# Own buffers for A22, A12 cast behind the copies, and a longer hand-written order at the FFN entry

## The chip, the core and the metric

The kernel runs on one core of one Trainium2 chip. The metric is the time of one execution on the device in microseconds (us), as the median of several runs. TensorE (PE in the profile) multiplies matrices, VectorE (DVE) and ScalarE (ACT) work element by element, GpSimd (POOL) here mostly issues DMAs, and SyncE (SP) issues most of the loads. Each engine takes its instructions in the order in which they were queued.

## What is computed

One layer of a diffusion backbone over 512 latent tokens of width 1024 with a context of 256 tokens: a modulated RMSNorm, one wide input projection, a pooling mixer and a bidirectional mLSTM, a gated sum, an output projection with a residual; then a second modulated RMSNorm, a SwiGLU feed-forward part with its own residual, and a last RMSNorm. The change lies in the feed-forward part (FFN), whose width is 2816, that is 22 tiles of 128:

```python
def _swiglu(h, w_in, w_out):
    g, u = jnp.split(h @ w_in, 2, axis=-1)
    return (jax.nn.silu(g) * u) @ w_out
...
        x = x + g2 * _swiglu(_modulate(x, norm_ffn[l], sh2, sc2), w_ffn_in[l], w_ffn_out[l])
```

All data are 32-bit floats. A product in that precision is made of three matmuls: each operand is split into a high part (a cast, on ACT) and a low part (operand minus high part, a subtraction on DVE), and the kernel adds high x high, high x low and low x high.

## The kernel before, in words

**Tiling.** Tokens lie along the free axis, 512 of them in two halves of 256. For each of the 22 FFN tiles j there are two weight tiles of 128 x 1024 (`wffi[2j]` for the gate, `wffi[2j+1]` for the up branch), eight k-tiles of 128 x 128 in each.

**Plain tiles and Strassen pairs.** FFN tiles 0, 1 and 2 are computed directly by the class `Half`, one half of the tokens at a time: 24 matmuls for `gate`, 24 for `up`, then `silu` on ACT, `product` on DVE, `high` (a cast on ACT) and `low` (a subtraction on DVE). From tile 3 on (`NP = 3`) gate and up tile are handled together as a 2 x 2 block matrix by the class `Pair`, with Strassen's scheme in Winograd's form: seven block products instead of eight. The gate tile holds A11 and A12 (its first and last four k-tiles), the up tile A21 and A22. The seven products use as stationary operands A11, S1, S2, A12, S3, S4 and A22, where S1 and S2 are sums made of A22, A21 and A11 (called sum12 here) and S3 and S4 are sums made of A11, A21, S2 and A12 (sum34). The token side (B11, N1, N2, B21, T3, B22, T4) is prepared once for all pairs. Each product is four k-tiles x three matmuls of 256 tokens, so 12 matmuls; a pair has 84.

**Making the weights of a pair.** The generator `prepare` (L1017) loads the up tile into a buffer `ur` (two of them) and the gate tile into a buffer `wr` (three) over SP's queue. Then come in program order: A11's cast and low part; sum12 (L1054, L1055 on DVE), its cast (L1044 on ACT, into `gh`) and low part (L1045 on DVE, into `gl`); A12; sum34 (L1061, L1062); its cast (into `wh`) and low part (into `wl`); A22. A11, A12 and A22 share the buffers `oh` (high) and `ol` (low), five of each, taken in turn, so a sixth tile waits for the product that reads the first. For A12 and A22 the low part is not made on DVE: ACT writes minus the high-part source into `ol` (L1038) and POOL issues a DMA that adds the weights from memory to it (L1039, an accumulating DMA). In two later pairs A11 goes that way too. An `ur` buffer is free for the next load when its A22 has been read, a `wr` buffer when A11, A12, sum12 and sum34 have read it.

**Order of the products.** A `Pair` has two generators. `front` gives A11 (whose result ACT copies from bank x to bank z, L1091), S1 (whose result ACT copies to a buffer q, L1095; this instruction is `copied`), S2 (added onto x; DVE then adds q, L1098) and A12 (added onto z). `back` gives S3, S4 and A22. S2 may not start before the copy of x to z, since it writes x. The function `run` strings pairs together; in a round the order on PE is A11, S1 of this pair, S3 of the pair before, S2 of this one, S4 before, A12 of this one, A22 before. Before the products of a round, `run` calls `made(after)`, which queues the whole preparation of the next pair.

**What sets the order.** The FFN entry (from L1349) is in a block whose order on PE, ACT and DVE is the program's, written out by hand. Outside such blocks a scheduler at build time orders each engine by program order, dependencies, buffers and its own estimates; DMA queues are always ordered by it. `issue_after(x)` adds an edge: what the block queues on x's engine comes behind x there, without a semaphore. In the entry, the hand-written block ends after A11 and S1 of pair 3 (called `third`) and its preparation; pair 4's preparation and products come from the scheduler.

**Where the pairs lie.** Pairs 3 to 7, then the output product for tiles 0 to 7 (`ffn_out`), then pairs 8 to 13 (`Even` and `Odd`), four `Out` pairs that apply Strassen's scheme to the output weights (their low parts are all made on DVE), pairs 14 to 21, and the rest of the output product. The buffers `oh` and `ol` also hold some weights of the output projection before the FFN (`wo`), of FFN tile 1 and of the last output product.

In the text pair n's operand is written A12(n), S3(n) and so on.

Of the kernel before, what the change touches and what calls it, by code (L numbers as in the profile page):

```python
# [10 lines left out]
F32 = mybir.dt.float32  # L11
# [6 lines left out]
P = 128  # L18
# [13 lines left out]
BUFS = {"a": 16, "ac": 8, "tmp": 7, "kq": 7, "q": 4, "E": 6, "Sp": 10, "m": 7, "pm": 4, "act": 16, "x1": 8, "oh": 5, "ol": 5}  # L32
# [18 lines left out]
def layer_kernel(ctx: ExitStack, tc, xT, cT, w0, w1, wv0, wv, wada_a, wada_b, par, crow, bg, wpool,  # L51
# [811 lines left out]
    for h in range(H):  # L863
# [13 lines left out]
        if h == H - 1:  # L877
            close_pool("att")
            close_pool("kqp")
            open_pool("late1", ("oh", "ol", "gh", "gl"))  # L880
            open_pool("late0", ("act",))
            for j in range(6):
                y_split(j)
# [66 lines left out]
    with tc.issue_after(ylow.ins):  # L950
        wo = {j: wload(wout[j], D, ("oh", "ol") if j < NW + 2 else None)[0] for j in range(NW, KT)}
# [65 lines left out]
    def prepare(p, wa, wb, n, turns, sent, behind=None):  # L1017

        a = tl("wr", [P, WMAX], F32, 3)[:, :2 * n]
        b = tl("ur", [P, D], F32, 2)[:, :2 * n]  # L1020
        p["loaded"] = nc.sync.dma_start(b, wb)
        nc.sync.dma_start(a, wa)

        def tiled(t):
            return t.rearrange("p (k c) -> p k c", c=P) if turns else t

        def parted(t):
            return [tiled(t)[:, e::2] for e in range(2)] if turns else [tiled(t[:, :n]), tiled(t[:, n:])]

        (a11, a12), (a21, a22) = parted(a), parted(b)  # L1030

        def direct(nm, w, dram):
            h, l = S("oh", F32R)[:, :n], S("ol", F32R)[:, :n]
            nc.scalar.copy(tiled(h), w)
            if nm not in sent:
                V.tensor_sub(tiled(l), w, tiled(h).bitcast(F32))  # L1036
            else:
                nc.scalar.activation(tiled(l), w, AF.Copy, scale=-1.0)  # L1038
                p["added"] = nc.gpsimd.dma_start(tiled(l), dram, accum_op=ALU.add)  # L1039
            p[nm] = ptiles(h, l, 0, n)  # L1040

        def summed(names, sg, h, l):
            h, l = h[:, :2 * n], l[:, :2 * n]
            nc.scalar.copy(h, sg)  # L1044
            p["low"] = V.tensor_sub(l, sg, h.bitcast(F32))  # L1045
            for e, nm in enumerate(names):
                p[nm] = ptiles(h, l, e * n, n)

        yield
        s12 = tl("sg", [P, D], F32, 2, LINE)[:, :2 * n]  # L1050
        s1, s2 = tiled(s12[:, :n]), tiled(s12[:, n:])
        direct("A11", a11, parted(wa)[0])
        with tc.issue_after(behind.ins) if behind else ExitStack():
            V.tensor_add(s1, a22, a21)  # L1054
        V.tensor_add(s2, s1, a11)  # L1055
        summed(("S1", "S2"), s12, wide("gh"), wide("gl"))
        yield
        direct("A12", a12, parted(wa)[1])
        yield
        s34 = tl("sg", [P, D], F32, 2, LINE)[:, :2 * n]  # L1060
        V.tensor_add(tiled(s34[:, :n]), a11, a21)  # L1061
        V.tensor_add(tiled(s34[:, n:]), s2, a12)  # L1062
        yield
        summed(("S3", "S4"), s34, *(tl(t, [P, WMAX], F32R, 2, LINE) for t in ("wh", "wl")))
        yield
        direct("A22", a22, parted(wb)[1])
        yield
# [3 lines left out]
    class Pair:  # L1071
# [5 lines left out]
        begun, f, behind = False, None, None  # L1077
# [5 lines left out]
        def prepare(self):  # L1083
            return prepare(self.p, wffi[2 * self.j], wffi[2 * self.j + 1], T, False, self.sent, self.behind)
# [128 lines left out]
    class Out(Pair):  # L1213
# [8 lines left out]
        def prepare(self):  # L1222
            w = [wffo[2 * self.j + e][:, self.c] for e in range(2)]
            return prepare(self.p, *w, (self.c.stop - self.c.start) // 2, True, self.sent)
# [28 lines left out]
    def made(it):  # L1253
        for _ in it.prepare():
            pass

    def run(items, also=lambda it: None):

        prev, casts[:] = None, []
        for it, after in zip(items, items[1:] + [None]):  # L1260
            f = it.f = it.f or it.front()
            if after:
                made(after)
            b = prev.back() if prev else iter(())
# [8 lines left out]
            if casts:  # L1273
                with tc.issue_after(it.copied.ins):
                    casts.pop().cast(0, 4)
# [6 lines left out]
            next(b, None)  # L1282
# [28 lines left out]
    for j in range(2):  # L1311
        d = ("oh", "ol") if j else "wide"
        pw.append((wload(wffi[2 * j], D, d)[0], wload(wffi[2 * j + 1], D, d)[0], act_tiles(j)))
# [35 lines left out]
    with tc.manual_schedule(engines={mybir.EngineType.PE, mybir.EngineType.Activation, mybir.EngineType.DVE}):  # L1349
# [41 lines left out]
        third = Pair(NP, NP)  # L1391
        p = third.prepare()
        next(p)
        next(p)
        e.silu()
        next(p)
# [4 lines left out]
        next(p)  # L1401
# [43 lines left out]
    turn = itertools.count(NP + 1)  # L1445
# [72 lines left out]
    for j, dst in enumerate((None, None, "wide", "wide", ("oh", "ol"), ("oh", "ol"), None, None)):  # L1518
# [117 lines left out]
```

## Time and profile before

| | |
|---|---|
| median of 3 runs | 883.52 us (882.77 to 883.98) |
| the profiled execution's own time | 883.43 us |
| span of its profile, first to last instruction | 881.6 us |
| PE busy | 870.8 us (99%), 6052 matmuls |
| DVE busy | 631.2 us (72%) |
| ACT busy | 454.2 us (52%) |
| POOL busy | 82.6 us (9%) |
| granted TensorE clock, mean | 0.999 |
| moved by DMA | 129.83 MB, mean 147 GB/s |

The span is 1.8 us shorter than the execution's own time; what lies around the span is not in the profile. In the timeline a row gives start and duration in us, engine, line and operation, output<-input by buffer name, and in brackets how long the engine was idle before it and who released it. A matmul's duration includes its way through the pipeline, so matmuls that follow each other without a gap overlap: what tells of a stall is the distance from one start to the next.

### The profile page before, as it was taken

To read this page: it belongs to the slowest core of one execution; us is meant where nothing else is said; L and a number is where in the kernel's file an instruction comes from. 1 tells how busy PE (TensorE), PEld (TensorE's weight loads), DVE (VectorE), ACT (ScalarE), POOL (GpSimd) and SP (SyncE) were. 2 spreads that over 40 slices of the span, in tenths; PEclk is the share of its full clock that TensorE was granted. 3 is DMA by queue.
4 is the path that set the end of the run, shared out by engine and by line. 5 is a ranking of instruction groups with operands and counts; after the bars stand their busy time and mean duration, and the time that the engine had idled before them with its cause. 6 is when DMAs were issued, how large, how long until landed. Compare 5 with 4: busy or idle time off the path is not lost.

```text
span 881.6 us, 15517 instructions
## 1 busy us (share of the span) xinstructions
PE 870.8 (99%) x6052; PEld 800.4 (91%) x6052; DVE 631.2 (72%) x1232; ACT 454.2 (52%) x867; POOL 82.6 (9%) x117
## 2 busy tenths in 40 slices
PE   9999999999999999999999999999999999999996
PEld 8689798899888998889988899999889999999996
DVE  5678677867876688767886667794376898786544
ACT  4464354455344453445454447674146768676431
POOL 0000010020000100000000000020011202322000
PEclk9999999999999999999999999999999999999999
DMA  9853021436252542434354740385476647998502
GB/s 352 326 194 112 25 72 60 169 106 181 72 185 91 152 158 83 148 112 140 127 162 130 266 141 1 89 211 133 131 207 171 150 108 213 219 227 204 168 1 96
DMA packets 45449, 129.83 MB, mean 147 GB/s; under 512 B 5024, under 2 KB 9408, under 8 KB 44352
## 3 DMA queue, kind: packets, MB, share of 16 engines
q1 hardware_dynamic: 37344, 112.59, 39.4%
q0 software_dynamic: 8032, 16.26, 9.5%
q8 instruction: 47, 0.77, 0.3%
q14 instruction: 26, 0.21, 0.1%
HBM read 120.94 MB, written 9.98 MB: 149 GB/s over the span
## 4 chain that ended last, share of the span: by engine, by line
PE 89%; DMA 3%; ACT 2%; DVE 2%; issue 2%; DVEq 0%; POOLq 0%; POOL 0%; SPq 0%; ACTq 0%
PE ps L191 12%; PE ps L192 12%; PE ps L193 12%; PE ps L201 8%; PE ps L199 8%; PE ps L198 8%; PE pat L351 3%; PE ps L582 3%; PE ps L583 3%; PE ps L584 3%; PE pat L192 2%; PE pat L193 2%; PE pat L191 2%; PE pat L796 2%; PE pat L797 2%
## 5 line engine op out<-in xcount | busy, mean ns | idle before, releaser
L161 ACT CAST wh<-wr 128x1024 fp32r<-128x1024 f32 (+2 forms) x70 | 71.8, 1025 | 83.0 <-PE ps L199 34.8
L162 DVE TENSOR_TENSOR wl<-wr,wh 128x1024 fp32r<-128x1024 f32 (+2 forms) x70 | 84.2, 1203 | 34.6 <-ACT wh L161 22.6
L198 PE MATMUL ps<-a,wh 128*128 128x512 f32 x272 | 106.6, 392 | 0.0
L199 PE MATMUL ps<-a,wh 128*128 128x512 f32 x272 | 106.3, 391 | 0.0
L201 PE MATMUL ps<-a,wl 128*128 128x512 f32 x272 | 68.0, 391 | 0.0
L199 PEld LDWEIGHTS ps<-a,wh 128*128 128x128 f32 x272 | 51.1, 188 | 10.2
L201 PEld LDWEIGHTS ps<-a,wl 128*128 128x128 f32 x272 | 50.9, 188 | 10.5
L198 PEld LDWEIGHTS ps<-a,wh 128*128 128x128 f32 x272 | 51.1, 188 | 10.1
L191 PE MATMUL ps<-act,wh 128*128 128x256 f32 (+1 forms) x155 | 51.5, 332 | 0.0
L193 PE MATMUL ps<-act,wl 128*128 128x256 f32 (+1 forms) x155 | 51.3, 331 | 0.0
L192 PE MATMUL ps<-act,wh 128*128 128x256 f32 (+1 forms) x155 | 51.3, 331 | 0.0
L191 PE MATMUL ps<-hp,gh 128*128 128x256 f32 x176 | 49.6, 282 | 0.8 <-ACT pat L1091 0.5
L193 PE MATMUL ps<-hp,ol 128*128 128x256 f32 x176 | 48.9, 278 | 0.7 <-DVE ol L1036 0.7
L1039 POOL DMA_DIRECT2D ol<-in_wffi x40 | 35.5, 897 | 145.9 <-ACT tmp L1126 62.9
L191 PE MATMUL ps<-hp,oh 128*128 128x256 f32 x176 | 49.0, 278 | 0.1
L192 PE MATMUL ps<-hp,gh 128*128 128x256 f32 x176 | 49.0, 278 | 0.0
L193 PE MATMUL ps<-hp,gl 128*128 128x256 f32 x176 | 48.9, 278 | 0.0
L192 PE MATMUL ps<-hp,oh 128*128 128x256 f32 x176 | 48.8, 277 | 0.0
L541 DVE SCALAR_TENSOR_TENSOR pb<-pb,crow_s 128x1024 f32<-128x1024 f32 x32 | 38.9, 1234 | 10.9 <-DMA pb<-in_wada_b 10.8
L796 PE MATMUL pat<-vh,Sp 128*128 128x258 f32 x144 | 41.1, 286 | 0.0
L797 PE MATMUL pat<-vl,Sp 128*128 128x258 f32 x144 | 40.7, 283 | 0.0
L798 PE MATMUL pat<-vh,Sp 128*128 128x258 f32 x144 | 40.7, 282 | 0.0
(421 smaller groups left out, 2870.3 us busy)
## 6 DMA issues: line engine op xcount, KB each, us to landing
wr<-in_w SPq DMA_DIRECT2D x42, 512.0 KB, 3.6
pb<-in_wada_b SPq DMA_DIRECT2D x32, 512.0 KB, 4.2
wr<-in_wffi SPq DMA_DIRECT2D x25, 512.0 KB, 4.2
ol<-in_wffi POOLq DMA_DIRECT2D x40, 256.0 KB, 6.0
ur<-in_wffi SPq DMA_DIRECT2D x19, 512.0 KB, 4.0
ada<-in_wada_a SPq DMA_DIRECT2D x8, 1024.0 KB, 10.4
wr<-in_wffo SPq DMA_DIRECT2D x16, 512.0 KB, 4.0
wr<-in_wout SPq DMA_DIRECT2D x8, 512.0 KB, 3.5
```

The costliest lines, as they stand in the source:

```text
L161: nc.scalar.copy(wh, raw[:, :n])
L162: V.tensor_sub(wl, raw[:, :n], wh.bitcast(F32))
L191: nc.tensor.matmul(dst, wh, ah, start=first and i == 0, stop=False, skip_group_check=on)
L192: nc.tensor.matmul(dst, wh, al, start=False, stop=False, skip_group_check=on)
L193: nc.tensor.matmul(dst, wl, ah, start=False, stop=last and i == n - 1, skip_group_check=on)
L198: nc.tensor.matmul(dst, wh, ah, start=first and i == 0, stop=False)
L199: nc.tensor.matmul(dst, wh, al, start=False, stop=False)
L201: nc.tensor.matmul(dst, wl, ah, start=False, stop=last and i == len(wparts) - 1)
L541: V.scalar_tensor_tensor(wa[:, :D], wa[:, :D], 0.5, crow_s, ALU.mult, ALU.mult, accum_out=mods[:, i:i + 1])
L796: nc.tensor.matmul(o, sh_, vh[:, s, :], start=n == 0, stop=False)
L797: nc.tensor.matmul(o, sh_, vl[:, s, :], start=False, stop=False)
L798: nc.tensor.matmul(o, sl_, vh[:, s, :], start=False, stop=n == len(srcs) - 1)
```

## The change

A22 gets two buffers of its own, `uh` and `ul`; `oh` and `ol` shrink from five to three. `prepare` becomes a class `Weights` whose steps can be called one by one. In `run`, of the next pair only the loads, A11 and sum12 (with cast and low part) are queued ahead of a round's products; A12, sum34 and A22 are queued behind `copied`, with an edge on ACT. A11's cast gets an edge behind the last sum12 cast. In the hand-written entry the order now goes further: pair 3's A12 is made before sum12, pair 4's sum12 before pair 3's sum34 cast, A22(3) last; on PE it fixes A11(3), S1(3), S2(3), A12(3), S3(3), A11(4), S1(4). `run` then starts with pair 4 and with `third` as the pair before. The edge `behind`, which held pair 5's sum12 behind a low part of pair 3, goes.

```diff
-BUFS = {..., "x1": 8, "oh": 5, "ol": 5}
+BUFS = {..., "x1": 8, "oh": 3, "ol": 3, "uh": 2, "ul": 2}
...
-        wo = {j: wload(wout[j], D, ("oh", "ol") if j < NW + 2 else None)[0] for j in range(NW, KT)}
+        wo = {j: wload(wout[j], D, {NW: ("oh", "ol"), NW + 1: ("uh", "ul")}.get(j))[0] for j in range(NW, KT)}
...
+    class Weights:
+        groups = (("A11", "low A11", "sum12", "S12", "low S12"), ("A12", "low A12"), ("sum34",), ("S34", "low S34"),
+                  ("A22", "low A22"))
...
+            p["loaded"] = nc.sync.dma_start(b, wb)
+            nc.sync.dma_start(a, wa)
...
+                if step in part:
+                    h, l = self.lows[step] = [S(t, F32R)[:, :n] for t in (("uh", "ul") if step == "A22" else ("oh", "ol"))]
+                    with tc.issue_after(casts12[-1].ins) if step == "A11" and casts12 else ExitStack():
+                        nc.scalar.copy(tiled(h), part[step])
...
+                    else:
+                        nc.scalar.activation(tiled(l), part[nm], AF.Copy, scale=-1.0)
+                        p["added"] = nc.gpsimd.dma_start(tiled(l), self.dram[nm], accum_op=ALU.add)
...
     def run(items, also=lambda it: None, prev=None):
...
-            if after:
-                made(after)
-            b = prev.back() if prev else iter(())
+            rest = prepare(after.weights) if after else iter(())
+            with tc.issue_after(it.copied.ins) if it.begun else ExitStack():
+                for _ in range(2):
+                    next(rest, None)
+            b = (prev.b or prev.back()) if prev else iter(())
...
-            if casts:
-                with tc.issue_after(it.copied.ins):
+            with tc.issue_after(it.copied.ins):
+                for _ in rest:
+                    pass
+                if casts:
                     casts.pop().cast(0, 4)
...
-            next(b, None)
+            if not (prev and prev.b):
+                next(b, None)
...
-        d = ("oh", "ol") if j else "wide"
-        pw.append((wload(wffi[2 * j], D, d)[0], wload(wffi[2 * j + 1], D, d)[0], act_tiles(j)))
+        ds = (("oh", "ol"), ("uh", "ul")) if j else ("wide", "wide")
+        pw.append((*(wload(wffi[2 * j + e], D, d)[0] for e, d in enumerate(ds)), act_tiles(j)))
...
-        third = Pair(NP, NP)
-        p = third.prepare()
-        next(p)
-        next(p)
+        third, second = Pair(NP, NP), Pair(NP + 1, NP + 1)
+        w = third.weights()
+        w("A11", "low A11", "A12", "low A12", "sum12", "S12", "low S12")
         e.silu()
-        next(p)
         e.mul()
         f = Half(2, HALF[1])
         f.gate()
         f.up()
-        next(p)
+        w("sum34")
+        w2 = second.weights()
         e.low()
         f.silu()
         f.product()
         banks += [PS() for _ in range(4)] + [PS("pat") for _ in range(4)]
-        fr = third.f = third.front()
-        third.begun = True
-        next(fr)
+        third.f = third.front()
+        next(third.f)
         f.high()
-        next(fr)
-        next(p)
-        next(p)
+        next(third.f)
+        w2("sum12")
+        w("S34")
+        next(third.f)
+        w("low S34")
+        w2("A11", "low A11", "S12")
+        next(third.f)
+        w2("low S12")
+        third.b = third.back()
+        next(third.b)
+        w2("A12", "low A12")
+        second.f = second.front()
+        second.begun = True
+        w("A22", "low A22")
+        next(second.f)
         f.low()
+        next(second.f)
...
-    plain = [third] + [Pair(j, next(turn)) for j in range(NP + 1, starts[0])]
-    plain[1].behind = third.p["low"]
-    for _ in run(plain).back():
+    plain = [second] + [Pair(j, next(turn)) for j in range(NP + 2, starts[0])]
+    with tc.issue_after(second.copied.ins):
+        w2("sum34", "S34", "low S34", "A22", "low A22")
+    for _ in run(plain, prev=third).back():
         pass
...
-    for j, dst in enumerate((None, None, "wide", "wide", ("oh", "ol"), ("oh", "ol"), None, None)):
+    for j, dst in enumerate((None, None, "wide", "wide", ("oh", "ol"), ("uh", "ul"), None, None)):
```

More of the change, by code (lines that the diff above doesn't have):

```diff
@@ L30 @@
 NG = 16
-BUFS = {"a": 16, "ac": 8, "tmp": 7, "kq": 7, "q": 4, "E": 6, "Sp": 10, "m": 7, "pm": 4, "act": 16, "x1": 8, "oh": 5, "ol": 5}
+BUFS = {"a": 16, "ac": 8, "tmp": 7, "kq": 7, "q": 4, "E": 6, "Sp": 10, "m": 7, "pm": 4, "act": 16, "x1": 8, "oh": 3, "ol": 3, "uh": 2, "ul": 2}
 LINE = 256
@@ L879, in layer_kernel @@
             close_pool("kqp")
-            open_pool("late1", ("oh", "ol", "gh", "gl"))
+            open_pool("late1", ("oh", "ol", "uh", "ul", "gh", "gl"))
             open_pool("late0", ("act",))
@@ L1015, in ptiles @@
         return [(h[:, o + i:o + i + P], l[:, o + i:o + i + P]) for i in range(0, n, P)]
[L1017 to L1047, printed above, removed]
-        yield
[L1050 to L1067, printed above, removed]
@@ L1069, in layer_kernel, with prepare @@
+    def prepare(made):
+        w = made()
+        yield
+        for steps in Weights.groups:
+            w(*steps)
+            yield
     banks = []
@@ L1076, in layer_kernel @@
         sent = ("A12", "A22")
-        begun, f, behind = False, None, None
+        begun, f, b = False, None, None
         def __init__(self, j, turn):
@@ L1081, in __init__, with weights @@
             self.p = {}
-        def prepare(self):
-            return prepare(self.p, wffi[2 * self.j], wffi[2 * self.j + 1], T, False, self.sent, self.behind)
+        def weights(self):
+            return Weights(self.p, wffi[2 * self.j], wffi[2 * self.j + 1], T, False, self.sent)
         def front(self):
@@ L1220, in __init__, with weights @@
             self.evens, self.c, self.into = evens, slice(c0 * P, c1 * P), od[c0]
-        def prepare(self):
+        def weights(self):
             w = [wffo[2 * self.j + e][:, self.c] for e in range(2)]
-            return prepare(self.p, *w, (self.c.stop - self.c.start) // 2, True, self.sent)
+            return Weights(self.p, *w, (self.c.stop - self.c.start) // 2, True, self.sent)
         @property
@@ L1253, in made, with run @@
     def made(it):
-        for _ in it.prepare():
+        for _ in prepare(it.weights):
             pass
-    def run(items, also=lambda it: None):
-        prev, casts[:] = None, []
+    def run(items, also=lambda it: None, prev=None):
+        casts.clear()
         for it, after in zip(items, items[1:] + [None]):
             f = it.f = it.f or it.front()
-            if after:
-                made(after)
-            b = prev.back() if prev else iter(())
+            rest = prepare(after.weights) if after else iter(())
[3 more added lines that the diff above has]
+            b = (prev.b or prev.back()) if prev else iter(())
             joint = isinstance(it, Out) and not isinstance(prev, Out)
@@ L1444, in layer_kernel @@
     starts = (8,)
-    turn = itertools.count(NP + 1)
-    plain = [third] + [Pair(j, next(turn)) for j in range(NP + 1, starts[0])]
-    plain[1].behind = third.p["low"]
-    for _ in run(plain).back():
+    turn = itertools.count(NP + 2)
+    plain = [second] + [Pair(j, next(turn)) for j in range(NP + 2, starts[0])]
+    with tc.issue_after(second.copied.ins):
+        w2("sum34", "S34", "low S34", "A22", "low A22")
+    for _ in run(plain, prev=third).back():
         pass
```

45 lines of the change are left out of this document (added).

## The prediction, written before the result was known

> **What bounds the kernel now.** I read the page first, then PE's waits, then PE's timeline row by row where pairs are entered.
>
> ```profile
> span 881.6 us, 15517 instructions
> ...
> PE 870.8 (99%) x6052; PEld 800.4 (91%) x6052; DVE 631.2 (72%) x1232; ACT 454.2 (52%) x867; POOL 82.6 (9%) x117
> ```
>
> PE is the bound: 870.8 of 881.6 us. The change takes no matmul away, so it can win only where PE stands still, and lose by making it stand still. PE's waits name these places:
>
> ```profile
> PE ps L193 <- DVE ol L1036: 0.7, 1, 0.7
> ...
> PE ps L191 <- ACT pat L1091: 0.5, 2, 0.3
> PE ps L191 <- ACT gh L1044: 0.4, 1, 0.4
> PE pat L193 <- DMA ol<-in_wffi: 0.3, 1, 0.3
> ```
>
> Three of the four are single waits at the FFN entry; L1091 is the copy of x to z, late twice. The view counts idle time after the modelled end of a matmul, so I measure from start to start in PE's timeline. First the entry:
>
> ```profile
> 570.43 0.28 PE L191 MATMUL pat<-hp,oh 128*128 128x256 f32 x1
> 570.55 0.28 PE L192 MATMUL pat<-hp,oh 128*128 128x256 f32 x1
> 571.09 0.40 PE L193 MATMUL pat<-hp,ol 128*128 128x256 f32 x1 [0.26 <-DMA ol<-in_wffi]
> 571.32 0.28 PE L191 MATMUL pat<-hp,oh 128*128 128x256 f32 x1
> ...
> 572.46 0.28 PE L192 MATMUL ps<-hp,oh 128*128 128x256 f32 x1
> 573.39 0.38 PE L193 MATMUL ps<-hp,ol 128*128 128x256 f32 x1 [0.65 <-DVE ol L1036]
> ...
> 574.54 0.28 PE L193 MATMUL ps<-hp,ol 128*128 128x256 f32 x1
> 575.18 0.39 PE L191 MATMUL ps<-hp,gh 128*128 128x256 f32 x1 [0.37 <-ACT gh L1044]
> ...
> 581.08 0.28 PE L192 MATMUL pat<-hp,oh 128*128 128x256 f32 x1
> 581.32 0.39 PE L193 MATMUL pat<-hp,ol 128*128 128x256 f32 x1
> ```
>
> Undisturbed, starts are 0.12 apart (570.43, 570.55). The four gaps are 0.54, 0.93, 0.64 and 0.24, so 0.42 + 0.81 + 0.52 + 0.12 = 1.87 too much. After a gap the next step is long too (571.09 to 571.32, 0.23, that is 0.11 too much), four times: 0.44. The entry loses 2.31 us: A12(3) waits for its accumulating DMA, A11(4) for its low part, S1(4) for its cast, A12(4) for its DMA. Then the late copies, on PE and on ACT:
>
> ```profile
> 748.52 0.28 PE L193 MATMUL ps<-bo,wl 128*128 128x256 f32 x1
> 748.97 0.39 PE L191 MATMUL ps<-hp,gh 128*128 128x256 f32 x1 [0.17 <-ACT pat L1091]
> ...
> 757.88 0.28 PE L193 MATMUL ps<-hp,wl 128*128 128x256 f32 x1
> 758.46 0.39 PE L191 MATMUL ps<-hp,gh 128*128 128x256 f32 x1 [0.30 <-ACT pat L1091]
> ```
>
> ```profile
> 748.00 0.64 ACT L1038 ACTIVATE ol<-wr 128x512 fp32r<-128x512 f32 x1
> 748.53 0.38 ACT L1091 COPY pat<-ps 128x256 f32<-128x256 f32 x1
> ...
> 757.49 0.65 ACT L1038 ACTIVATE ol<-wr 128x512 fp32r<-128x512 f32 x1
> 758.02 0.39 ACT L1091 COPY pat<-ps 128x256 f32<-128x256 f32 x1
> ```
>
> Both times ACT negates A12 (L1038) directly ahead of the copy, and S2 stands until the copy has ended. The gaps are 0.45 and 0.58; less 0.12 and plus 0.11 for the long restart, 0.44 + 0.57 = 1.01 us. The second has a sequel, seen in the starts of S4, one round of 84 matmuls apart:
>
> ```profile
> 759.98 0.28 PE L191 MATMUL pat<-hp,wh 128*128 128x256 f32 x1
> ...
> 769.86 0.28 PE L191 MATMUL pat<-hp,wh 128*128 128x256 f32 x1
> ...
> 779.47 0.28 PE L191 MATMUL pat<-hp,wh 128*128 128x256 f32 x1
> ```
>
> The round after the gap took 9.88 us (117.6 ns a matmul, 1.41 us a product), the next 9.61 (114.4 ns): 0.27 us more, with no wait named. I count that to the late copy.
>
> **The change, part by part.**
>
> *Behind the copies.* In a round ACT now gets A12, sum34's cast and A22 of the next pair behind `copied`, so L1038 can't stand ahead of L1091 any more. Gain 1.01 + 0.27 = 1.28 us. The moved work has time: A12 of the next pair is now made a round ahead, because it no longer shares buffers with an A22 that is still being read. The instructions that move are two casts, the negation and its POOL issue for each of A12 and A22; their landing is wanted nine or more products (12 us) later.
>
> *The entry.* The DVE and ACT instructions stay the same in number; only order and place change. I build it from these rows (timeline of PE, DVE and ACT; the groups of the tile sg):
>
> ```profile
> 672.00 0.28 PE L191 MATMUL pat<-hp,wh 128*128 128x256 f32 x1
> ```
>
> ```profile
> 672.27 0.43 DVE L1098 TENSOR_TENSOR pat<-ps,tmp 128x256 f32<-128x256 f32 x1 [1.04 <-PE ps L193]
> ```
>
> ```profile
> 569.49 1.05 ACT L1044 CAST wh<-sg 128x1024 fp32r<-128x1024 f32 x1
> ```
>
> ```profile
> L1054 DVE TENSOR_TENSOR sg<-ur x23: 550/692/694, 562.7 to 797.0; 128x512 f32<-128x512 f32 x19, 128x384 f32<-128x384 f32 x4
> ...
> L1044 ACT CAST gh<-sg x23: 829/1052/1068, 564.2 to 798.8; 128x1024 fp32r<-128x1024 f32 x19, 128x768 fp32r<-128x768 f32 x4
> L1045 DVE TENSOR_TENSOR gl<-sg,gh x23: 950/1225/1227, 565.3 to 799.9; 128x1024 fp32r<-128x1024 f32 x19, 128x768 fp32r<-128x768 f32 x4
> ```
>
> A12(3): its cast and negation now follow A11's cast, ahead of sum12's cast and of the Silu that stood before them. Earlier by these (1.05 and more), its landing no longer comes 0.42 late. Its wait goes. On PE S2(3) ends and A12(3) starts at 570.43 as before; S3(3) follows at 571.84, and its third matmul, the first that reads the low part, at 572.08. DVE's new order puts L1098 ahead of that low part, and L1098 starts 0.27 after S2's end (672.00, 672.27): 570.70 + 0.43 + 1.23 = 572.36. So S3(3) waits 0.28, with the long restart 0.4 us: a new stall. Queued behind L1098 on DVE are low S34(3), low A11(4) and low S12(4). PE then has A11(4) at 573.65, S1(4) at 575.06, S2(4) 576.5, S4(3) 577.9, A12(4) 579.3, A22(3) 580.7, A11(5) 582.1, S1(5) 583.5. DVE has low A11(4) (0.69, as L1054's size) by 573.05 and low S12(4) by 574.28: in time, both old waits go.
>
> On ACT S34(3)'s cast starts at 569.49 as before. Starts of 512 wide operations are 0.53 apart (748.00, 748.53), so A11(4)'s cast starts at 570.54, S12(4)'s 571.07 to 572.12; the Silu of A12(3)'s result takes as long as a copy (0.38), to 572.5. Then cast, negation (0.64, from L1038's row), cast, negation: A12(4) is negated by 573.67, A22(3) by 574.73. These landings then decide, and the load of pair 5's `ur`, which waits for A22(3): before, that load was issued between 571 and 573, now at 574.73. From the DMA issues in 571 to 573, 573 to 574.5 and 574.5 to 577 us, and from the tile ol:
>
> ```profile
> ur<-in_wffi SPq DMA_DIRECT2D x1, 512.0 KB, 4.1
> ```
>
> ```profile
> ol<-in_wffi POOLq DMA_DIRECT2D x1, 256.0 KB, 7.3
> ```
>
> ```profile
> ol<-in_wffi POOLq DMA_DIRECT2D x2, 256.0 KB, 8.4
> ur<-in_wffi SPq DMA_DIRECT2D x1, 512.0 KB, 7.0
> ```
>
> ```profile
> DMA to landing us min/median/max: 4.0/6.0/9.4
> ```
>
> The slow ones (7.0 to 8.4) ran with three accumulating DMAs and three loads within 4 us; in the new order there are two and one within 1.1 us, so I take the median, 6.0, and for `ur` 5.0, between 4.1 and 7.0 and nearer the row with less beside it. A12(4): 573.67 + 6.0 = 579.67 against its third matmul at 579.5, a stall of 0.2. A22(3): 580.7 against 580.9, none. S12(5): `ur` at 579.73, two sums of 0.69, cast 1.05: 582.2 against 583.5; low part 583.4 against 583.75, none. What it costs at the bounds stands with the rivals. The entry's sum: -2.31 + 0.4 + 0.2 = -1.7 us.
>
> By the Trainium skill, "DMA: Bandwidth & Descriptors", section on the anatomy of a DMA on the gpsimd path, such a DMA takes 2.0 us plus its bytes over 436 GB/s, an estimated 2.6 us for 256 KB; by that no landing could be late, the sum would be 0.2 better and the first rival would have no chance. The trace's own 4.0 to 9.4 speaks against it, so the rival stays.
>
> *Buffers.* `wffi[3]`, one output projection tile and one tile of the last chunk move to `uh`/`ul`: nothing, since both are cast several products before use; if the cover failed it would be one cast and one subtraction, about 1.1 us (half of 1.05 + 1.23). The total of buffers is the same. Edge on A11's cast: nothing; that cast is wanted a round later.
>
> *Sum.* 883.43 (profiled execution) - 1.28 - 1.7 = 880.45; the median of before lies 0.09 above that execution, so 880.5.
>
> **Rivals.**
>
> *The DMAs come late.* Moving A22(3) to the end also moves the `ur` load and bunches two accumulating DMAs with it. With the slow rows: A12(4) lands at 573.67 + 7.3 = 580.97, 1.5 late; A22(3) at 574.73 + 8.4 = 583.1, against 582.4 by then, 0.7 late; S12(5)'s low part at 585.4 against 585.95, not late. With two restarts 2.4, and 0.4 for S3: 2.8 against 2.31, the entry loses 0.5, and with the copies' 1.28 the time is 882.7. For it: A12(4) took 7.3 before. Against it: fewer DMAs beside it.
>
> *The copies stay late.* The scheduler may put something else ahead of L1091: sum12's cast (1.05) and A11 still precede the copies in program order. Then 1.28 is not won, and the time is 881.8.
>
> *Slower.* The same mechanism, but recurring: sum12's cast, queued ahead of the copies, waits for a late `ur`, and ACT waits with it.
>
> ```profile
> DVE sg L1054 <- DMA ur<-in_wffi: 12.0, 10, 2.2
> ```
>
> In ten rounds DVE does wait for `ur`. A gap of 0.45 to 0.58 a time, 0.5 with restart, in 12 of the 18 pair rounds is 6 us, giving 886.5; from 6 rounds on it eats the 3.0 us won, from 10 on it is slower by over 0.2%. Against it: before, program order had that cast ahead as well, and the copies were late for another instruction.
>
> **How the numbers follow.** 0.2% is 1.77 us, about what a measurement of this kernel can tell from no change: 881.75 is the border. Forecast (880.5): 0.52. DMAs late (882.7): 0.18. Copies late (881.8, at the border): 0.14, half of it faster, half same. Both of these, or no effect at all (883 to 884): 0.08, same. Slower: 0.08. Faster 0.52 + 0.07 and 0.03 from a mild form of the first rival, 0.62; same 0.30; slower 0.08. The range: from 879.0 (no new stall, 0.6 less; ten products of the entry at 1.37 in place of 1.41, 0.4; and half a microsecond by which the three runs of before differ from their median) to 883.2, between the first rival and no effect.
>
> **What would show it.** Right: no wait of PE for ol L1036, gh L1044 or L1091; a wait for wl L1045 of about 0.3 in S3(3), at about 572; S4 to S4 about 9.6 us in every round of the last pairs. Wrong: waits of PE for the DMA into ol or ul between 579 and 584, or for gh or gl at S1(5); L1091 late behind L1044; the time above 881.75.

## The result and the profile after

| | median | lowest to highest, runs | profiled execution, its span |
|---|---|---|---|
| before | 883.15 us | 882.77 to 883.98, 4 | 883.43, 881.6 us |
| after | 895.75 us | 893.10 to 896.17, 4 | 893.10, 891.3 us |

The change made the kernel slower: ratio 1.0135, 95% interval 1.0114 to 1.0156. The prediction said 880.5 us, faster. The page's header and the same waits of PE as before, now of the changed kernel (columns: us in total, times, longest):

```profile
span 891.3 us, 15503 instructions
...
PE 874.6 (98%) x6052; PEld 802.9 (90%) x6052; DVE 629.7 (71%) x1232; ACT 451.4 (51%) x867; POOL 83.4 (9%) x117
```

```profile
PE ps L191 <- ACT pat L1112: 3.2, 4, 1.5
PE ps L191 <- DVE tmp L1150: 1.8, 1, 1.8
PE ps L193 <- DMA ul<-in_wffi: 1.6, 1, 1.6
...
PE ps L193 <- DMA ol<-in_wffi: 0.2, 1, 0.2
```

The work is the same, 6052 matmuls. The entry's three single waits are gone, as predicted. The late copy of x to z (L1112, formerly L1091) is not: four waits of 3.2 us in all instead of two of 0.5, and three other waits stand beside it, of 1.8, 1.6 and 0.2 us. Behind the copies stand ACT's and DVE's waits; the last row is ACT's of the kernel before:

```profile
DVE sg L1064 <- DMA ur<-in_wffi: 19.4, 11, 3.4
```

```profile
ACT gh L1053 <- DVE sg L1065: 28.3, 13, 4.8
```

```profile
ACT gh L1044 <- DVE sg L1055: 12.9, 6, 3.3
```

sum12 now waits 19.4 us for `ur` (12.0 before), and its cast, `gh`, holds ACT for 28.3 us (12.9 before).

Where the time lies is read from PE's timeline, from the first matmul of each stage to the first of the next (us). "Own" is the first experiment below, the kernel before with nothing but the new buffers.

| stage | before | after | own |
|---|---|---|---|
| normalization and first tiles (e.gate to tile 2) | 23.55 | 24.54 | 24.54 |
| entry and pairs 3 to 7 | 50.73 | 50.65 | 49.81 |
| pairs 8 to 13 | 55.47 | 58.81 | 57.33 |
| `Out` pairs | 28.97 | 29.30 | 31.46 |
| pairs 14 to 21 | 81.63 | 84.54 | 83.34 |
| last output product | 47.66 | 49.56 | 49.56 |

The differences of before and after are 0.99, -0.08, 3.34, 0.33, 2.91 and 1.90: 9.4 us; the stages left out between them are equal within 0.01. Everything ahead of these stages took 0.8 more in this execution, with the same instructions, and what lies behind them 0.5 less: 9.7 us, the difference of the spans. This execution was the fastest of the four, and what the others lost beyond it, up to the 12.6 us of the medians, no trace shows. Stage times here and below are of one execution each and differ by more than a microsecond where no change bears on them: in e9 below, the kernel before with nothing but an unused tile, pairs 14 to 21 took 80.45 us. So the entry, for which the change was written out by hand, came out even, and all the loss is in stages to which the prediction gave a gain or nothing.

### The profile page after: what moved, and what is told of

Read it like the earlier page. It is cut to its first block, busy times and chain, and to the rows that moved or that the text cites. A ratio compares the mean times of both kernels' runs of the same rounds, so it can differ in the third digit from the quotient of the medians.

```text
span 891.3 us, 15503 instructions
## 1 busy us (share of the span) xinstructions
PE 874.6 (98%) x6052; PEld 802.9 (90%) x6052; DVE 629.7 (71%) x1232; ACT 451.4 (51%) x867; POOL 83.4 (9%) x117
## 4 chain that ended last, share of the span: by engine, by line
PE 83%; DMA 7%; DVE 3%; issue 3%; ACT 2%; POOL 0%; SPq 0%; DVEq 0%; ACTq 0%; POOLq 0%
PE ps L191 11%; PE ps L193 11%; PE ps L192 11%; PE ps L201 8%; PE ps L199 8%; PE ps L198 8%; PE ps L582 3%; PE ps L583 3%; PE ps L584 3%; PE pat L351 2%; PE pat L796 2%; PE pat L797 2%; PE pat L798 2%; DMA ada<-in_wada_a 2%; PE pat L192 2%
## 5 line engine op out<-in xcount | busy, mean ns | idle before, releaser
L1053 ACT CAST gh<-sg 128x1024 fp32r<-128x1024 f32 (+1 forms) x23 | 23.3, 1013 | 32.9 <-DVE sg L1065 28.3
L191 PEld LDWEIGHTS ps<-hp,gh 128*128 128x128 f32 x176 | 33.1, 188 | 4.0 <-ACT pat L1112 4.0
L583 PE MATMUL ps<-wl,a 128*128 128x256 f32 (+1 forms) x128 | 36.3, 283 | 0.0
L584 PE MATMUL ps<-wh,a 128*128 128x256 f32 (+1 forms) x128 | 36.2, 283 | 0.0
```

The source lines that it names most:

```text
L191: nc.tensor.matmul(dst, wh, ah, start=first and i == 0, stop=False, skip_group_check=on)
L583: nc.tensor.matmul(acc[:, :n], ah, wl, start=False, stop=False)
L584: nc.tensor.matmul(acc[:, :n], al, wh, start=False, stop=kk == KT - 1)
```

## The experiments

Each line gives the median with the lowest, the highest and the number of runs, and the ratio to the kernel before on the same chip with its interval. In expectations "late copies" are waits of PE for L1091 or its successors.

### One part at a time

**e1, own buffers alone**: the kernel before with the change's `BUFS`, A22 in `uh`/`ul`, and the three other tiles moved there.

```diff
-            h, l = S("oh", F32R)[:, :n], S("ol", F32R)[:, :n]
+            h, l = [S(t, F32R)[:, :n] for t in (("uh", "ul") if nm == "A22" else ("oh", "ol"))]
```

> The kernel before with one part of the change: A22 in two buffers of its own, oh and ol cut from five to three; order and entry as before. Theory 1 (the buffers): with two own buffers the cast of A22(n) cannot start before the product of A22(n-2) has ended; so the up tile's buffer ur is freed late, its load lands late (DVE waited 19.4 us for it in the changed kernel, 12.0 before), and ACT, held at sum12's cast, copies x to z late. Then this part alone is 6 to 12 us slower than before, with PE waits for the copy L1091. Theory 2 (the order in run): this part alone changes less than 2 us. Theory 3 (the entry): less than 2 us.

**e2, the order alone**: the kernel before with the run's new order (A12, sum34, A22 behind `copied`) and both edges, shared buffers, old entry.

```diff
-            if after:
-                made(after)
...
+            with tc.issue_after(it.copied.ins):
+                for _ in rest:
+                    pass
```

> The kernel before with another part alone: in run, of the next pair only A11 and sum12 are queued ahead of a round's products, A12, sum34 and A22 behind the copies, with the edges on ACT (A11's behind sum12's cast too); five shared buffers and the entry as before. Theory 2 (the order): queueing A22 behind the copies frees ur late, whatever buffer A22 uses, so this part alone is 6 to 12 us slower, with late copies. Theory 1 (the buffers): within 2 us of before, and the two late copies of before (1.0 us) go. Theory 3 (the entry): as theory 1.

**e3, the entry alone**: the changed kernel with five shared buffers and the old order in `run`.

```diff
-            with tc.issue_after(it.copied.ins) if it.begun else ExitStack():
-                for _ in range(2):
-                    next(rest, None)
+            if after:
+                made(after)
```

> The changed kernel with five shared buffers again and the old order in run (the whole preparation of the next pair queued ahead of a round's products, no edges): only the longer hand-written entry is left of the change. Theory 3 (the entry): moving A22(3) to the end delays pair 5's ur and every later one with it, so this alone is 6 to 12 us slower. Theories 1 and 2: it costs or gains at most 2 us, all of it before 600 us, and the later pair rounds are as before.

**e4, everything but the own buffers.**

```diff
-"oh": 3, "ol": 3, "uh": 2, "ul": 2}
+"oh": 5, "ol": 5}
```

> The whole change but for the buffers: A22 shares five oh and ol with A11 and A12 again. Theory 1 (the buffers): 8 to 12 us of the loss go, within 2 us of before. Theory 2 (the order): it stays 6 us or more slower than before. If both are needed for the loss, this, the buffers alone and the order alone all stay within 3 us of before.

| | median (range, runs) | ratio (interval) |
|---|---|---|
| e1 own buffers | 892.11 (891.05 to 893.59, 4) | 1.0103 (1.0087 to 1.0119) |
| e2 order | 884.52 (881.81 to 886.92, 10) | 1.0012 (0.9998 to 1.0026) |
| e3 entry | 883.79 (881.61 to 886.40, 10) | 1.0001 (0.9986 to 1.0015) |
| e4 order and entry | 885.06 (881.81 to 886.49, 10) | 1.0019 (1.0007 to 1.0032) |

Of the 12.6 us the own buffers alone cost 8.1 by the medians and 9.1 by the ratio; order and entry, alone or together, cost about 1 us or nothing. The own buffers and the rest, each by itself (e1 and e4), make 9 to 11 us; the 1 to 3 us that are missing come only with both together, and no run separates them. PE's waits of e1 (in its code the copy is still L1091):

```profile
PE ps L191 <- ACT pat L1091: 3.0, 4, 1.3
...
PE ps L191 <- DVE tmp L1129: 1.0, 1, 1.0
```

So a change of buffers made the copies late, in an otherwise old program. How, is seen in one round of the timelines. Before (SP, ACT, DVE):

```profile
675.99 0.33 SPq L1021 DMA_DIRECT2D ur<-in_wffi  x1
...
685.92 0.33 SPq L1021 DMA_DIRECT2D ur<-in_wffi  x1
```

```profile
674.81 0.62 ACT L1034 CAST oh<-ur 128x512 fp32r<-128x512 f32 x1
...
681.70 1.05 ACT L1044 CAST gh<-sg 128x1024 fp32r<-128x1024 f32 x1 [2.32 <-PE ps L192]
...
684.74 0.62 ACT L1034 CAST oh<-ur 128x512 fp32r<-128x512 f32 x1 [0.35 <-ACT tmp L1133]
```

```profile
680.05 0.69 DVE L1054 TENSOR_TENSOR sg<-ur 128x512 f32<-128x512 f32 x1 [1.69 <-DMA ur<-in_wffi]
680.77 0.69 DVE L1055 TENSOR_TENSOR sg<-sg,wr 128x512 f32<-128x512 f32 x1
```

And e1, the same round:

```profile
677.02 0.33 SPq L1021 DMA_DIRECT2D ur<-in_wffi  x1
...
687.73 0.33 SPq L1021 DMA_DIRECT2D ur<-in_wffi  x1
```

```profile
675.85 0.61 ACT L1034 CAST uh<-ur 128x512 fp32r<-128x512 f32 x1
...
683.86 1.05 ACT L1044 CAST gh<-sg 128x1024 fp32r<-128x1024 f32 x1 [4.81 <-DVE sg L1055]
684.82 1.05 ACT L1044 CAST wh<-sg 128x1024 fp32r<-128x1024 f32 x1
...
686.55 0.62 ACT L1034 CAST uh<-ur 128x512 fp32r<-128x512 f32 x1
...
690.52 0.37 ACT L1091 COPY pat<-ps 128x256 f32<-128x256 f32 x1
```

```profile
682.35 0.69 DVE L1054 TENSOR_TENSOR sg<-ur 128x512 f32<-128x512 f32 x1 [1.83 <-DMA ur<-in_wffi]
```

Read it as a loop. A22's cast and negation free an `ur` buffer (675.85 to 677.00); SP loads the next up tile into it (677.02); sum12 waits for that load (682.35); sum12's cast waits for sum12 and holds ACT (683.86); behind it in ACT's queue stand the next A22's cast, 686.55, which frees the next `ur` (687.73), and the copy, 690.52, for which S2 waits. This turn of the loop takes 687.73 - 677.02 = 10.71 us, while PE's undisturbed round takes 9.61 (S4 to S4 in the kernel before, 769.86 to 779.47). Before, the same turn took 685.92 - 675.99 = 9.93 us, and its cast `gh` was released by PE, not by sum12, which had ended 0.24 us earlier (680.77 + 0.69 against 681.70): the loop had that much slack. With five shared buffers, taken in turn, A22(n) gets the buffer of A11(n-1), the first product of the round in which A22(n) is made; with two of its own it gets that of A22(n-2), the last product of that round, six products later. So A22's cast came 1.04 us later (675.85 against 674.81), the next load took 5.33 us to be read instead of 4.06 (why, is not shown), and the loop lost its slack. Whether the late cast or `ur` is the link that counts, this run does not tell.

### Deeper or shallower rings

**e5, three `uh`/`ul` and two `oh`/`ol`** on e1; ten tiles still. **e6**, the same on the whole change.

```diff
-"oh": 3, "ol": 3, "uh": 2, "ul": 2}
+"oh": 2, "ol": 2, "uh": 3, "ul": 3}
```

> The kernel before with A22's own buffers alone, but three of them and two for A11 and A12, ten tiles in all as before. In the own-buffers run with two, A22's cast of pair n waited for A22's product of pair n-2 and came 1.4 us later in the round than in the kernel before; ur's load, sum12 and its cast followed late. Theory 1 (the depth of A22's own ring starts that chain): A22's cast waits for pair n-3, long past, so most of the 9 us are gone: 883 to 886.5 us. Rival (the loss comes from the shorter ring of A11 and A12, or from A22 having a ring of its own at all): as slow as with two, 891 to 894 us, or slower still, since A11 and A12 have two buffers in place of three.

> The whole change, with three buffers for A22 and two for A11 and A12. Theory 1: the part of the loss that belongs to the ring (some 10 of 12 us) goes, 884 to 887.5 us; A22 of pair 3 still waits some 2 us for its accumulating DMA in the entry. Rival (the order behind the copies and the entry need A11's and A12's three buffers): 891 us or more.

e5: 890.68 us (889.13 to 892.57, 5), 1.0083 (1.0070 to 1.0096). e6: 889.24 us (888.27 to 891.82, 5), 1.0072 (1.0059 to 1.0084). Both lie above what theory 1 expected, e6 6.5 us under the changed kernel and e5 1.4 under e1. PE's waits of e5, and ACT's:

```profile
PE pat L193 <- DMA ol<-in_wffi: 5.0, 7, 2.0
...
PE ps L191 <- ACT gh L1044: 0.9, 1, 0.9
```

```profile
ACT oh L1034 <- PE pat L192: 8.3, 10, 2.3
```

The late copies are nearly gone (one wait of 0.2), as are all of VectorE's waits for `ur`; in their place A12's cast waits for A12's product of the pair before, its accumulating DMA is issued late, and PE waits for that seven times, 5.0 us. The normalization's stage is back at 23.56 us. So depth matters, but this run moved the shortage from one ring to the other and could not decide.

**e13 to e15** free 4 KB in each partition by five `tmp` buffers in place of seven. e13 is that alone, the control; e14 is e1 with three buffers in both rings; e15 is e1 with three `ur`. e14 to e16 have the padding of e10, below.

```diff
-"tmp": 7
+"tmp": 5
...
-        b = tl("ur", [P, D], F32, 2)[:, :2 * n]
+        b = tl("ur", [P, D], F32, 3)[:, :2 * n]
```

> The kernel before with five `tmp` buffers in place of seven: the control for the three runs beside it, which need the 4 KB of each partition that this frees. No theory of the change bears on it; its time is the base of the others. Where five `tmp` buffers bind, its rounds are longer: 883 to 888 us.

> The kernel before with own buffers for A22, three of them and three for A11 and A12, five `tmp` buffers, and the late `act` tiles at 192 past a multiple of 256. Theory (each ring of its own is too short: two for A22 hold up A22's cast, two for A11 and A12 hold up A12's DMA): no late copies and no waits for A12's DMA, so the time of the control within 1.5 us. Rival (a ring of A22's own costs whatever its depth): 5 us or more over the control.

> The kernel before with own buffers for A22 (two), three `ur` buffers in place of two, five `tmp` buffers, and the late `act` tiles at 192. Theory of the chain (A22's cast waits for the product of pair n-2, so ur's buffer comes free late, so sum12 and its cast wait for ur's DMA, so the copy behind that cast is late): with a third `ur` the load no longer waits for A22's cast; VectorE's waits of 1 us and more for ur and the late copies go, and the time is the control's plus 1 us (the normalization's stage) to 3 us. Rival (the late cast of A22 holds up ScalarE's queue by itself, whatever ur does): 5 us or more over the control, the copies as late as with two.

| | median (range, runs) | ratio (interval) |
|---|---|---|
| e13 control | 884.49 (882.78 to 888.89, 12) | 1.0013 (1.0000 to 1.0025) |
| e14 three and three | 884.50 (883.05 to 887.87, 12) | 1.0009 (0.9997 to 1.0021) |
| e15 three `ur` | 885.33 (884.28 to 886.12, 12) | 1.0019 (1.0011 to 1.0028) |

This decides. With three buffers in each ring A22's own buffers cost nothing over the control; with two and a third `ur` they cost 0.8 us by the medians, and e15's normalization stage, still 24.44 us against 23.56, accounts for that. In neither run does VectorE wait for `ur` at all. PE's waits of e15:

```profile
PE pat L191 <- ACT pat L1092: 0.7, 1, 0.7
PE ps L191 <- DVE tmp L1130: 0.6, 1, 0.6
...
PE pat L193 <- DMA ol<-in_wffi: 0.3, 1, 0.3
PE ps L191 <- ACT pat L1092: 0.3, 1, 0.3
```

A22's cast waits for the same product in e15 as in e1 (ACT waits for PE there 11 times, 6.7 us), yet in place of e1's four late copies (3.0 us) S2 waits for one, 0.3 us; the 0.7 is in the entry. So what counts is the loop through `ur`, not the late cast by itself. One of these three expectations was missed: e14's profiled run, the slowest of its twelve, still has three late copies (2.4 us), so the depth of the ring alone does not end them in every execution.

### The place of the `act` tiles

In the build's memory plan the two extra ring names move all tiles behind them: the late `act` tiles, which the last output product reads, start 192 bytes past a multiple of 256 in the kernel before and 128 past one in after, e1, e5 and e6. **e9** and **e10** change nothing but that, by an unused tile behind the weight buffers; **e12** does it to the whole change. **e11** moves T3, S3's token operand, from 208 to 192 past a multiple of 256.

```diff
+            tl("pad", [P, 48], F32)
             open_pool("late0", ("act",))
```

(48 words in e9, 16 in e10 and e12.)

```diff
-for o in [NEXT + i * D + i // 6 * 4 for i in range(7)]
+for o in [NEXT + i * D for i in range(7)]
```

> The kernel before with 192 bytes of padding, unused, behind the weight buffers: nothing changes but the place of the late `act` tiles, which the output products of the last pairs read: they start 128 bytes past a multiple of 256 instead of 192, as they do in the changed kernel and in every run with A22's own buffers. Theory (their address sets the matmul spacing of the last output product: 118.5 ns in each of the four runs with own buffers, 113.4 in each of the five with shared ones): the last stage goes from 47.7 to 49.6 us and the run from 883.3 to 885.2 us; the spacing of the products that read `act` is 118.5 ns there. Rival (a wider spacing that a late stall leaves behind): no change, 883.3 us, spacing 113.4 ns.

> The kernel before with own buffers for A22 (two) and 64 bytes of padding behind the weight buffers, so that the late `act` tiles start 192 bytes past a multiple of 256 again. Address theory: the last stage 47.7 us instead of 49.6 and the run 892.1 - 1.9 = 890.2 us, still with the late copies. Rival: 892.1 us, the last stage 49.6.

> The kernel before with T3, which S3's products read, 16 bytes lower, so that it starts 192 bytes past a multiple of 256 as the other moving operands do, and not 208. In every run so far S3's products had a spacing of 118.7 ns where all others of the pairs had 113.3 to 115. Address theory: S3's spacing goes to 113 to 114 ns, some 19 x 12 matmuls x 5 ns = 1.2 us less: 882.1 us. Rival (the spacing belongs to S3's place in the round or to its weights): 118.7 ns still and 883.3 us.

> The whole change with 64 bytes of padding behind the weight buffers. Address theory: 895.8 - 1.9 = 893.9 us, the last stage 47.7 us. Rival: 895.8 us.

| | median (range, runs) | ratio (interval) | last stage |
|---|---|---|---|
| e9 before, `act` at 128 | 885.05 (883.60 to 886.46, 12) | 1.0012 (1.0002 to 1.0023) | 49.56 us |
| e10 own, `act` at 192 | 891.54 (890.18 to 894.10, 6) | 1.0086 (1.0070 to 1.0103) | 47.65 us |
| e11 before, T3 at 192 | 883.64 (880.46 to 887.95, 12) | 0.9999 (0.9982 to 1.0016) | 49.05 us |
| e12 after, `act` at 192 | 891.25 (889.47 to 893.19, 6) | 1.0084 (1.0067 to 1.0100) | 50.02 us |

The windows view of PE shows it in one row each (stretch, its length, PE's busy time and count of matmuls, granted clock, DMA share, GB/s): before, after, e9 and e10, all in the last output product.

```profile
840.00:850.00 10.00, 10.00 (x91) 1.00 0.01 2
```

```profile
840.00:850.00 10.00, 10.00 (x87) 1.00 0.15 48
```

```profile
840.00:850.00 10.00, 10.00 (x87) 1.00 0.01 2
```

```profile
840.00:850.00 10.00, 10.00 (x91) 1.00 0.08 32
```

At 128 a matmul every 118.6 ns, at 192 every 113.3, with the granted clock at 1.00 in all four: 1.9 us over the stage, without a wait that any view names. e9 confirms it in the median (1.7 us more), e10 in the stage, though its median is only 0.6 us under e1's (1.5 by the ratios). But the address is not all: in e11, e12 and e18 (below) the stage was long again, 49.0 to 50.0 us with `act` at 192, at a spacing of 117 to 118 ns.

e11 shows both, T3's address and this second spacing. The first matmuls of one S3 and of the product after it, before, then e11 with a later row:

```profile
678.80 0.28 PE L191 MATMUL ps<-hp,wh 128*128 128x256 f32 x1
...
680.23 0.28 PE L191 MATMUL ps<-hp,gh 128*128 128x256 f32 x1
```

```profile
678.72 0.28 PE L191 MATMUL ps<-hp,wh 128*128 128x256 f32 x1
...
680.08 0.28 PE L191 MATMUL ps<-hp,gh 128*128 128x256 f32 x1
...
758.17 0.39 PE L191 MATMUL ps<-hp,gh 128*128 128x256 f32 x1 [0.55 <-ACT pat L1091]
```

S3's twelve matmuls took 1.43 us with T3 at 208 and 1.36 at 192, and so in every FFN pair's round of e11 from 577 to 757 us: 113.3 ns a matmul, as in the products beside it. The address theory holds for S3 too. From the stop at 758.17 on, behind a late copy, all products of e11 run at 117 to 118 ns, through the pairs and the last stage up to 864 us, and take back what was won. In the kernel before the same spacing sets in at the stop at 758.46, also behind a late copy, and ends with the next S3, at 768.47: it is the round of 9.88 us in the prediction. In e12 and e18 it sets in at PE's last wait ahead of the last stage (832.02 and 826.49) and stays through the stage. So it comes behind a stop of PE, and in these pair rounds S3 with T3 at 208 ended it, which e11 no longer has; not every stop brings it (the one at 584.12 in the changed kernel, shown below, does not). What makes it stays open. e11's times spread most of all runs, 880.46 to 887.95; that it wins where no stop sets this spacing off is possible, and not shown.

e12's median fell by 4.5 us where 1.9 were expected; its profiled run, at 892.95, shows the long stage and the late copies, so where the rest comes from is not shown.

### Does the rest of the change win anything?

**e7** and **e8** are e3 and e4 with A22 of pair 3 made 8 us earlier, where ACT stands idle; **e16** is the whole change with three and three buffers and that; **e17** is the control with three `ur`; **e18** is e8 with five `tmp` and three `ur`.

```diff
         e.silu()
+        w("A22", "low A22")
...
         second.begun = True
-        w("A22", "low A22")
```

> Five shared buffers, the old order of the run, and the new entry with A22 of pair 3 cast and sent in the 1.3 us in which ScalarE stands idle behind the first silu of the last half, some 8 us earlier than in the entry run. If the new entry's only fault is that A22's accumulating DMA lands late, its 1.35 us of waiting at 580 go, as does the wait for ur of pair 5: 881.5 to 883 us. Rival: the earlier cast pushes the last half's casts back and nothing is won: 883.5 to 885 us.

> The whole change with five shared buffers, and A22 of pair 3 cast early as in the run beside it. If the two gains of the change (the entry's waits, 1.7 us; the late copies, 1.3 us) add up once the own buffers and the late A22 are gone: 880 to 882 us. Rival (casts queued behind the copies cost as much in the rounds as they win): 883 to 885 us.

> The whole change with three buffers for A22 and three for A11 and A12, five `tmp` buffers, A22 of pair 3 cast early in the entry, and the late `act` tiles at 192. If the change's two gains (the entry's waits, the late copies) are real once no ring is short: 1 to 2.5 us under the control. Rival (the order behind the copies puts new waits in the place of the old): the control within 1.5 us, or over it.

> The kernel before with three `ur` buffers and five `tmp` buffers. In the kernel before VectorE waits 12.0 us in ten rounds for ur's DMA, and two copies are 0.3 and 0.2 us late. If those waits for ur are what makes the copies late there too: the copies' waits go, 0.5 to 1 us under the control (884.5 us) and level with the kernel before or just under it, 882.5 to 884 us. Rival (VectorE's waits for ur are hidden in the kernel before): the control's time.

> The whole change but with five shared buffers, A22 of pair 3 cast early in the entry, three `ur` and five `tmp` buffers: the version that the runs point to. If the entry's and the copies' waits are worth what the prediction put on them (3.0 us together) once no load of ur is late: 880.5 to 882 us. Rival (the new order's own waits take it back, as in the runs before): 883.5 to 885.5 us.

| | median (range, runs) | ratio (interval) | entry and pairs 3 to 7 | pairs 14 to 21 |
|---|---|---|---|---|
| before | | | 50.73 us | 81.63 us |
| e2 order | as above | | 50.49 | 80.82 |
| e7 entry, early A22 | 883.81 (882.08 to 885.24, 11) | 1.0007 (0.9999 to 1.0016) | 49.97 | 82.34 |
| e8 change, shared, early A22 | 885.08 (883.15 to 888.96, 12) | 1.0021 (1.0009 to 1.0034) | 49.17 | 83.20 |
| e16 change, three and three | 884.75 (882.65 to 887.12, 12) | 1.0010 (0.9998 to 1.0022) | 50.45 | 80.64 |
| e17 control, three `ur` | 884.20 (883.51 to 887.09, 11) | 1.0011 (1.0002 to 1.0021) | 50.47 | 80.49 |
| e18 change, shared, three `ur` | 883.30 (881.08 to 885.78, 11) | 0.9997 (0.9986 to 1.0008) | 49.01 | 82.34 |

The expectations of a gain were all missed. In its own stage the entry's gain is seen in two runs: e18 takes 1.72 us out of it and e8 1.56, below every run with the old entry (49.8 us and more); e7 takes 0.76 and e16, with A22 in its own ring, 0.28. It does not reach the end. PE's waits of e8 and of e18 show what stands later:

```profile
PE ps L191 <- DVE tmp L1150: 2.3, 3, 0.8
...
PE ps L191 <- ACT pat L1112: 0.8, 2, 0.4
```

```profile
PE ps L191 <- DVE tmp L1150: 1.6, 1, 1.6
```

L1150 is the sum that VectorE makes of S3's result; A22's product overwrites the bank that it reads, and now waits for it. In the kernel before no such wait is named. Two of e8's three stand behind a late `ur` again, now in VectorE's queue:

```profile
780.32 0.69 DVE L1064 TENSOR_TENSOR sg<-ur 128x512 f32<-128x512 f32 x1 [3.31 <-DMA ur<-in_wffi]
781.05 0.69 DVE L1065 TENSOR_TENSOR sg<-sg,wr 128x512 f32<-128x512 f32 x1
781.65 0.42 DVE L1150 TENSOR_TENSOR tmp<-ps,tmp 128x256 f32<-128x256 f32 x1
```

With a third `ur` (e18) those are gone, and so are VectorE's waits for it. What is left there is one long wait, behind a low part of the last output product, whose cast waited for a load that the change does not touch:

```profile
823.46 1.05 ACT L180 CAST gh<-wr 128x1024 fp32r<-128x1024 f32 x1 [2.36 <-DMA wr<-in_wffo]
```

That cast's wait was 0.8 us in the kernel before, 2.5 in the changed one and 0.7 to 2.4 in e2, e4, e7, e8, e16 and e18. The profiled execution of e18, the slowest of its eleven, also ran its last stage at the wider spacing behind that wait, 49.03 us in place of 47.66. So one execution's end moves by as much as the entry wins. No version beat the kernel before by more than the noise. e18 is level with it and 0.9 us under its control e17, with intervals that overlap: a gain of about a microsecond from the order and the entry is possible, and not shown.

## Why the prediction was wrong, point by point

**The late copies, -1.28: not won, because of the buffers.** The text said that the moved work has time because A12 "no longer shares buffers with an A22 that is still being read". It took sharing for the constraint and did not count what the ring gives to A22: its own buffer came free six products later than the shared one. Instead of two late copies the changed kernel had four, 3.2 us of waits. The sign named for it, L1091 late behind L1044, is what the traces show, with other work between the two (683.86 and 690.52 in e1). From there ran the loop that the third rival described (sum12's cast, held by a late `ur`, holds ACT). That rival had the mechanism, though not that A22's ring sets it off, and a chance of 0.08. Its price, 6 us over the rounds, is near the 6.6 us that the stages of pairs 8 to 21 lost, by luck: it counted 12 stops of 0.5 us, and there were four, of 0.4 to 1.5, with stretches of wider spacing behind them. It set 3.0 us won against that, which were not won, and had no term for the 2.9 us of the two other stages. The reason against it, that the cast stood ahead of the copies before too, was true and beside the point: in the round shown of the kernel before `gh` was released by PE, and had slack. For the order by itself the step was half right: in e2 no wait of PE for the copy is left. But a gain isn't shown: pairs 14 to 21 take 80.82 us there, 0.81 less than before, and 80.45 in e9 with the old order, and e2's median is above the kernel before.

**"Buffers: nothing": the step that failed, wrong by all that e1 lost, 8 to 9 us.** The prediction asked of the three other tiles that move whether they are cast in time. It did not ask of A22 itself which product its new slot waits for, and so had no term for the loop. The bound given, about 1.1 us if the cover failed, is what one part of it cost. Columns below as in the timelines before; first before, then after:

```profile
526.03 0.48 DVE L974 SCALAR_TENSOR_TENSOR tmp<-x,sc,pat 128x256 f32<-128x256 f32 x1
```

```profile
526.92 0.69 DVE L175 TENSOR_TENSOR ul<-wr,uh 128x512 fp32r<-128x512 f32 x1
527.53 0.42 DVE L231 TENSOR_TENSOR tmp<-tmp,tmp 128x256 f32<-128x256 f32 x1
527.87 1.26 DVE L974 SCALAR_TENSOR_TENSOR tmp<-x,sc,pat 128x256 f32<-128x256 f32 x3
```

`wffi[3]`, two tiles wide, must wait for both halves of the output projection tile that it shares `uh` with, and its last low part (526.92) stands ahead of the normalization on VectorE: 0.99 us. The rest are the loop and the 1.9 us of the last stage, which come from the new place of the `act` tiles; of that the profile of before shows only that S3's matmuls are wider apart than the others.

**The entry, -1.7: right piece by piece but for one DMA.** All three old waits went. S3(3)'s stall, forecast 0.4, came to about 0.2 us (two steps of 0.23 in place of 0.12), with no wait named; A12(4), forecast 0.2 late, was in time. A22(3), forecast in time, was late, the first of the signs named for a wrong forecast:

```profile
573.86 0.28 PE L191 MATMUL pat<-hp,wh 128*128 128x256 f32 x1
574.09 0.39 PE L193 MATMUL ps<-hp,wl 128*128 128x256 f32 x1
```

```profile
576.58 0.87 POOL L1080 DMA_DIRECT2D ul<-in_wffi  x1
```

```profile
582.21 0.28 PE L192 MATMUL ps<-hp,uh 128*128 128x256 f32 x1
584.12 0.38 PE L193 MATMUL ps<-hp,ul 128*128 128x256 f32 x1 [1.63 <-DMA ul<-in_wffi]
```

From issue to the matmul that it released are 7.5 us; the forecast put 6.0, the median, and the first rival 8.4. The mechanism was right and the landing was mis-sized. By the Trainium skill, "DMA: Bandwidth & Descriptors", anatomy of a DMA on the gpsimd path, 2.6 us was the estimate; the trace disagrees, as it did before. Where that DMA was moved early (e7, e8, e16, e18), the stage's gain was 0.76, 1.56, 0.28 and 1.72, against 1.7 forecast. But the sum's last step, that a gain in one stage is a gain at the end, is not borne out: in the medians it is not to be seen.

**A slip in the text ahead of the prediction:** the edge `behind` held pair 4's sum12, not pair 5's.

## What to carry to other kernels

A buffer of one's own is not a freer buffer: work out for each tile which earlier reader its new slot waits for, under the old ring and under the new, and follow what that tile's own reading frees. Where a load, a sum, a cast and the next load form a loop through one engine's queue, compare the loop's length with the round's; a loop with a quarter of a microsecond of slack goes unseen in the profile of before and takes over when one link moves by a microsecond. A new buffer name also moves every tile behind it: look at the matmul spacing in stages that the change does not touch, and product by product, since a mean over a whole run mixes stretches of different spacing.

## What the runs showed of the hardware

The start address of a matmul's moving operand changed its spacing at an unchanged granted clock of 1.00. As means of the steps in PE's timeline, without stops: 113.3 to 113.6 ns for the last output product at 192 bytes past a multiple of 256 (before, e4, e8), 118.6 to 118.7 at 128 (after, e1, e5, e6, e9), 118.8 to 118.9 for S3 with T3 at 208 (in all of these), and 113.3 for S3 with T3 at 192 (e11, up to 757 us). By the Trainium skill, "SBUF — State Buffer", Operand start alignment, a 4-byte operand may start at any multiple of 4; that section says of itself that it is about legality and not speed, and these runs show the speed. Beside it there is a spacing of 117 to 118 ns with the operand at 192, also at a granted clock of 1.00 (87 matmuls in the 10 us in which the kernel before has 91). In the traces shown it sets in behind a stop of PE (758.46 in the kernel before, 758.17 in e11, 832.02 in e12, 826.49 in e18) and can last through a whole stage; in the kernel before it ended with the next S3, whose operand starts at 208. Why, the profile does not say.
